# Latent attention: value products in fp32 on the two column halves of the array, in batches of four blocks, and divisors from sums made by GpSimd

## The chip, the cores and the metric

The kernel runs on one core of a Trainium2 chip. The metric is the device time of one execution in microseconds (us). Before the change it is 2091.34 us, the median of 3 runs (2090.69 to 2093.28).

TensorE (PE) does the matrix products, with its weight loads listed apart (PEld); VectorE is DVE, ScalarE is ACT, GpSimd is POOL, and SP issues most of the DMAs.

## The reference

A decoder trunk of two layers over 1024 positions, width 1024, all in fp32. Layer 0 mixes with multi-head latent attention of 12 heads, layer 1 with sliding-window attention; both have four memory cross-attention heads beside them and a dense MLP behind. The change touches the attention of layer 0 only:

```python
def causal_dense_attention(q, k, v):          # 12 heads, q and k 96 wide, v 64 wide
    ...
        sc = jnp.einsum('bqhd,bkhd->bhqk', q_blk, k,
                        preferred_element_type=jnp.float32) * scale
        mask = k_idx[None, :] <= t_idx[:, None]
        sc = jnp.where(mask[None, None], sc, NEG)
        p = jax.nn.softmax(sc, axis=-1).astype(v.dtype)
        return jnp.einsum('bhqk,bkhd->bqhd', p, v)
```

## The kernel before

**Tiling.** Scores are made transposed, keys on the partitions: a block (G, k) holds the 128 keys of tile k against up to 512 queries of half G (queries 0 to 511 for G = 0, 512 to 1023 for G = 1), less the columns that causality rules out. A head has twelve blocks: eight for G = 1 (512 columns for k = 0 to 4, then 384, 256 and 128) and four for G = 0 (512, 384, 256, 128). The list `blocks` gives their order, `seq` strings the heads together, and one loop over `n` issues for each n the scores of one block, pieces of the next heads' row maxima, and the value products of blocks that lie a few steps back (`LV` = 3 and `LB` = 5).

**Scores.** `scores` (matmuls at L1042) makes three fp32r products for each block (high by high, high by low, low by high), so that two fp32r numbers stand for one fp32. The row maximum of the head, made ahead by `row_max` (L909, one fp32r pass, reduced on DVE at L916) and turned by `max_row` (L888), rides along as a 97th row. DVE then adds the causal mask to the diagonal 128 columns of eight of the twelve blocks (L1050), and ACT takes the exponential into `p` (L1052).

**Values and divisors.** `values` (L1072) multiplies `v` by `p` and adds over k in one PSUM bank for each (head, G), `pso`. The weights are 128 wide: 64 columns of v and 64 of ones, so that row 64 of the result is the sum of the probabilities, the divisor. Blocks of G = 1 (and k = 3 of G = 0) are done "whole", in fp32, with `vf` (filled by `v_full`, a DVE copy at L1145). Blocks k = 0, 1, 2 of G = 0 are done as three fp32r products with `vh`, `vl` (made by `v_tiles`, ACT at L1014 and DVE at L1015) and with `ph`, `pl`, which ACT (L99) and DVE (L100) split from `p`. When a (head, G) is complete, ACT copies 65 rows out (L1098), and two SP DMAs send 64 of them to `qn` and the divisors to `den`.

**Division.** After heads 5, 9 and 10 `rc_split` takes reciprocals of `den` (L1131), sends them through DRAM (`rcd`, L1132) and has them broadcast to `rb` (`rc_pair`, L1124). `rc_mul` multiplies `qn` by them on DVE (L1141). For groups 0 and 1 these DMAs are issued by POOL, for group 2 by SP. The last head is divided straight from PSUM by `last_o` (L1111, L1112). Behind the loop `wo_phase` begins the output projection (`pswo`, L109 to L111), with its first four steps calling `last_o` for G = 0.

**Order.** A tile scheduler sets the order on each engine from the order of the program; on the chip each engine runs its list in order. PSUM has eight banks: six one-bank slots ("m"), for `pss`, `pso`, `psxt` and the short `psx`, and one two-bank slot ("x") for the `psx` of row tiles 4 to 7.

Of the kernel before, what the change touches and what calls it, by code (L numbers as in the profile page):

```python
# [19 lines left out]
P = 128  # L20
# [35 lines left out]
def trunk(  # L56
# [970 lines left out]
    probs, po_, masked = {}, {}, []  # L1027

    def width(G, k):
        return 512 - max(0, k - 4 * G) * P  # L1030

    def scores(h, G, k):

        qh, ql, kh, kl = bufs_[h % 3]
        c0 = 512 - width(G, k)
        ks = slice(k * P, (k + 1) * P)
        qs = slice(G * 512 + c0, G * 512 + 512)
        diag = k >= 4 * G
        ps = ps1(f"pss{h}_{G}_{k}")[:, c0:]

        def mm(o, a, b, **kw):
            return lambda: nc.tensor.matmul(o, a, b, skip_group_check=True, **kw)  # L1042

        mms = [mm(ps, kh[:, ks], qh[:, qs], start=True, stop=False)]
        mms.append(mm(ps, kh[:, ks], ql[:, qs], start=False, stop=False))
        mms.append(mm(ps, kl[:, ks], qh[:, qs], start=False, stop=True))

        def then():
            if diag:
                masked[0:1] = [nc.vector.tensor_tensor(ps[:, 0:P], ps[:, 0:P], dmaskT, ALU.add).ins]  # L1050
# [1278 lines left out]
```

## Time and profile before

| what | value |
|---|---|
| device time, median of 3 | 2091.34 us |
| profiled execution, span | 2089.8 us |
| latent attention of layer 0 in the span | about 233 to 434 us |
| one head in the middle of it | about 16.5 us |
| PE busy in that stretch of 201 us | 198.09 us |
| DVE, ACT, POOL busy in it | 156.58, 126.35, 14.00 us |

The span runs from the first to the last instruction of one profiled execution; the median is 1.5 us above it. A line of the profile names the source line, the engine, the operation, the tiles written and read and their shapes, how many instructions there were, their busy time and the mean of one, and the idle time just ahead of them with what ended it. In a timeline each row gives a start, a duration, and how many instructions of one kind in a row it groups; matmuls overlap their neighbours in such a row, so what a matmul costs is the distance between starts, not the duration printed.

### The profile page before, as it was taken

The numbers are of one execution on the slowest core, as the hardware profiler recorded it, in microseconds if no ns is written. First come the engines' busy times: TensorE is split into PE (matmuls) and PEld (weight loads), VectorE is DVE, ScalarE is ACT, GpSimd is POOL, SyncE is SP. The second block draws the span as 40 slices with busy tenths as digits, with TensorE's granted clock in tenths as the row PEclk, the third lists the DMA queues.
The fourth block names the chain that finished last, engine by engine and source line by source line (L and its number), as shares of the span: only waits on it lengthen the run. The fifth ranks groups of instructions, "written<-read, shape, count | busy, mean of one in ns | idle before, by whom it ended". The sixth has DMA issues, their size and how long they took to land.

```text
span 2089.8 us, 28906 instructions
## 1 busy us (share of the span) xinstructions
PE 2072.6 (99%) x9744; PEld 1692.2 (81%) x9744; DVE 1475.7 (71%) x2978; ACT 1109.4 (53%) x2396; POOL 148.6 (7%) x265
## 2 busy tenths in 40 slices
PE   9999999999999999999999999999999999999998
PEld 6988777778888888888888888778888888888887
DVE  8766778775977777976558534666977776976565
ACT  7554466666745544444445435766755544444453
POOL 1001001000000000000001133420000000000000
PEclk9999999999999999999999999999999999999999
DMA  6302223342444546944433534542344446944332
GB/s 225 104 1 77 63 65 93 105 149 81 142 152 150 167 152 233 332 129 152 143 118 108 146 101 124 142 130 84 128 152 164 161 144 233 324 146 156 117 121 91
DMA packets 182228, 292.86 MB, mean 140 GB/s; under 512 B 17739, under 2 KB 72128, under 8 KB 182080
## 3 DMA queue, kind: packets, MB, share of 16 engines
q1 hardware_dynamic: 175584, 272.60, 41.5%
q0 software_dynamic: 5168, 15.80, 2.1%
q10 hardware_dynamic: 1328, 2.63, 0.4%
q8 instruction: 76, 1.25, 0.2%
q14 instruction: 72, 0.59, 0.1%
HBM read 187.60 MB, written 81.44 MB: 129 GB/s over the span
## 4 chain that ended last, share of the span: by engine, by line
PE 94%; DVE 3%; ACT 1%; DMA 1%; issue 1%; SPq 0%; POOL 0%; DVEq 0%; ACTq 0%
PE psy L1903 6%; PE psy L1901 6%; PE psy L1902 6%; PE psu L1565 5%; PE psu L1564 5%; PE psu L1563 5%; PE psz L1903 4%; PE psz L1902 4%; PE psz L1901 4%; PE psv L1565 4%; PE psv L1564 4%; PE psv L1563 4%; PE pso L1072 3%; PE pss L1042 3%; PE pswo L109 3%; PE pswo L111 3%
## 5 line engine op out<-in xcount | busy, mean ns | idle before, releaser
L99 ACT ACTIVATE g<-i 128x512 fp32r<-128x512 f32 x79 | 49.9, 631 | 104.6 <-PE psy L1902 51.8
L1901 PE MATMUL psy<-g 128*128 128x512 f32 x256 | 100.1, 391 | 0.0
L1902 PE MATMUL psy<-g 128*128 128x512 f32 x256 | 99.8, 390 | 0.0
L1903 PE MATMUL psy<-g 128*128 128x512 f32 x256 | 99.8, 390 | 0.0
L1052 ACT ACTIVATE p<-pss 128x512 f32<-128x512 f32 (+2 forms) x144 | 68.7, 486 | 58.5 <-DVE pss L1050 50.0
L100 DVE TENSOR_TENSOR g<-i,g 128x512 fp32r<-128x512 f32 x79 | 55.5, 702 | 51.0 <-ACT g L99 51.0
L1072 PE MATMUL pso<-p,vf 128*128 128x512 f32 (+3 forms) x214 | 87.8, 492 | 0.0
L99 ACT ACTIVATE i<-mr 128x512 fp32r<-128x512 f32 x78 | 47.8, 629 | 73.2 <-PE psy L1902 24.5
L99 ACT ACTIVATE uh<-i 128x512 fp32r<-128x512 f32 x66 | 41.6, 630 | 82.4 <-PE psz L1902 38.4
L100 DVE TENSOR_TENSOR uh<-i,uh 128x512 fp32r<-128x512 f32 x66 | 45.6, 691 | 47.3 <-ACT uh L99 47.2
L916 DVE CUSTOM_DVE_ANT_0 psx<-psx,wide 128x1024 f32<-128x1024 f32 (+6 forms) x88 | 66.7, 760 | 14.6 <-PE psx L909 14.4
L1903 PE MATMUL psz<-g 128*128 128x512 f32 x192 | 74.8, 389 | 0.0
L1901 PE MATMUL psz<-g 128*128 128x512 f32 x192 | 74.8, 389 | 0.0
L1902 PE MATMUL psz<-g 128*128 128x512 f32 x192 | 74.8, 389 | 0.0
L1462 ACT ACTIVATE mr<-mr,gcol 128x256 f32<-128x256 f32 (+1 forms) x160 | 63.9, 477 | 13.9 <-DMA mr<-in_mlp_w_up_dram 13.9
L100 DVE TENSOR_TENSOR i<-mr,i 128x512 fp32r<-128x512 f32 x78 | 53.7, 688 | 24.7 <-ACT i L99 24.7
L1903 PEld LDWEIGHTS psy<-g 128*128 128x128 f32 x256 | 48.1, 188 | 9.9
L1902 PEld LDWEIGHTS psy<-g 128*128 128x128 f32 x256 | 48.1, 188 | 9.8
L1901 PEld LDWEIGHTS psy<-g 128*128 128x128 f32 x256 | 48.1, 188 | 9.8
L1783 DVE TENSOR_TENSOR mqq<-mqf,mqq 128x512 f32<-128x512 f32 x64 | 43.2, 687 | 18.2 <-DMA mqf<-in_mlp_w_down_dram 18.1
L1462 ACT ACTIVATE d<-d,gcol 128x256 f32<-128x256 f32 x128 | 53.6, 499 | 0.1
L2158 ACT ACTIVATE sp<-sp,sst 128x257 f32<-128x257 f32 (+1 forms) x96 | 46.5, 488 | 13.0 <-DVE sst L2156 12.7
(674 smaller groups left out, 6855.4 us busy)
## 6 DMA issues: line engine op xcount, KB each, us to landing
i<-hd SPq DMA_DIRECT2D x154, 256.0 KB
hd<-uh SPq DMA_DIRECT2D x76, 256.0 KB
hd<-ul SPq DMA_DIRECT2D x76, 256.0 KB
mr<-in_mlp_w_up_dram SPq DMA_DIRECT2D x36, 512.0 KB
hd<-x SPq DMA_DIRECT2D x72, 256.0 KB
mr<-hd SPq DMA_DIRECT2D x70, 256.0 KB
d<-in_mlp_w_up_dram SPq DMA_DIRECT2D x32, 512.0 KB
mqf<-in_mlp_w_down_dram SPq DMA_DIRECT2D x32, 512.0 KB
```

Of the source, the lines that this page charges most:

```text
L99: a = nc.scalar.activation(hi, src, AF.Copy)
L100: d = nc.vector.tensor_tensor(lo, src, f32(hi), ALU.subtract)
L916: nc.vector.tensor_tensor_reduce(o, o, k, -1.0, least, ALU.add, ALU.min, accum_out=m)
L1052: masked[1:] = [nc.scalar.activation(p[:, c0:], ps, AF.Exp, scale=SC).ins]
L1072: mms.append(lambda: nc.tensor.matmul(o, a, b, skip_group_check=True, **kw))
L1462: nc.scalar.activation(w[:, k, :], w[:, k, :], AF.Copy, scale=g_mlp[layer][:, k0 + k : k0 + k + 1])
L1563: nc.tensor.matmul(ps, wh[:, k, :], xh[:, k, :], start=p in (1, 2, 5) and k == 0, stop=False, skip_group_check=True)
L1564: nc.tensor.matmul(ps, wh[:, k, :], xl[:, k, :], start=False, stop=False, skip_group_check=True)
L1565: nc.tensor.matmul(ps, wl[:, k, :], xh[:, k, :], start=False, stop=k == 3, skip_group_check=True)
L1901: nc.tensor.matmul(ps, ah[:, j, :], bh, start=start, stop=False, skip_group_check=True)
L1902: nc.tensor.matmul(ps, ah[:, j, :], bl, start=False, stop=False, skip_group_check=True)
L1903: nc.tensor.matmul(ps, al[:, j, :], bh, start=False, stop=k == NP - 1, skip_group_check=True)
```

## The change

`p` stays in fp32 for all blocks and is kept in ten buffers. `values` takes four blocks at a time: each block's columns are cut into quarters of 256, a quarter's weights are the 64 columns of `v` alone, and the two quarters of a half go to the left and the right 64 columns of the array (`g`), taken in turns. One PSUM bank holds the head's output. The divisors come from `acc`: POOL copies and adds the blocks' probabilities (ten adds and two copies for a head), and `sums` multiplies the two halves of `acc` by 64 columns of ones. ACT copies them out and three SP DMAs send them to `den`. `evac` copies the output once for a head, 128 by 512, and issues two SP DMAs. `v_tiles`, `v_full`, the splits `ph` and `pl`, and the lags `LV` and `LB` are gone, the order in `blocks` is another, the DMAs of `rc_split` and `rc_pair` are all issued by SP, and `last_o` works on both column halves in two steps in place of four.

```diff
-    blocks = [(1, 0), (0, 0), (1, 4), (0, 1), (1, 5), (0, 2), (1, 6), (0, 3), (1, 7), (1, 1), (1, 2), (1, 3)]
+    blocks = [(1, 0), (0, 0), (1, 5), (0, 1), (1, 4), (0, 2), (1, 1), (1, 6), (1, 2), (0, 3), (1, 7), (1, 3)]
+    BATCH = 4
+    def quarters(G, c0=0):
+        return [(part ^ G, max(c0, part * 256), part * 256 + 256) for part in range(2) if c0 < part * 256 + 256]
...
-            p = at.tile([P, 512], F32, tag="p", bufs=5, name=f"p{h}_{G}_{k}")
-            if whole(h, G, k):
-                probs[(h, G, k)] = p
-                return
-            ph = at.tile([P, 512], F32R, tag="ph", bufs=3, name=f"ph{h}_{G}_{k}")
-            pl = at.tile([P, 512], F32R, tag="pl", bufs=3, name=f"pl{h}_{G}_{k}")
-            split(p[:, c0:], ph[:, c0:], pl[:, c0:])
+        p = at.tile([P, 512], F32, tag="p", bufs=10, name=f"p{h}_{G}_{k}")
...
+            if c0:
+                nc.gpsimd.tensor_copy(a[:, :c0], q[:, :c0])
+        nc.gpsimd.tensor_tensor(a[:, c0:], p[:, c0:], (a if q is None else q)[:, c0:], ALU.add)
...
-            mm(po[:, c0:], vfs[h % 2][:, k, :], probs.pop((h, G, k))[:, c0:], start=first, stop=last)
+            for g, a, b in quarters(G, col0(G, k)):
+                todo[g].append((b - a, po[g * 64 : g * 64 + 64, base + a % 256 : base + a % 256 + b - a], v[:, k, h * 64 : h * 64 + 64], p[:, a:b], g, begun))
...
+        while todo[0] or todo[1]:
+            for t in todo:
+                if t:
+                    _, o, w, r, g, begun = t.pop(0)
+                    nc.tensor.matmul(o, w, r, start=g not in begun, stop=True, skip_group_check=True)
...
-            on = at.tile([65, 512], F32, tag="on", bufs=2, name=f"on{h}_{G}")
-            nc.scalar.activation(on, po[0:65], AF.Copy)
+        on = at.tile([P, 512], F32, tag="on", bufs=2, name=f"on{h}")
+        nc.scalar.activation(on, po, AF.Copy)
...
+            nc.tensor.matmul(sp[0:64].rearrange("p (a c) -> p a c", c=256), ones, acc4[:, 0:4:3, :], start=True, stop=True, skip_group_check=True)
+            nc.tensor.matmul(sp[64:128], ones, acc[:, 256:768], start=True, stop=True, skip_group_check=True)
...
-            (nc.sync if c == 2 else nc.gpsimd).dma_start(out=rb[e * 64 : e * 64 + 64, :], in_=rc_d[c][2 * j + e, halves[i]].partition_broadcast(64))
+            nc.sync.dma_start(out=rb[e * 64 : e * 64 + 64, :], in_=rc_d[c][2 * j + e, halves[i]].partition_broadcast(64))
...
+        if n % BATCH == 1 and n > BATCH:
+            values(seq[n - 1 - BATCH : n - 1])
+            if j == 1 and h < H:
+                evac(h - 1)
+            if j == 5 and h:
+                sums(h - 1)
```

Three places show what the scheduler makes of it. Names hold the head, the half and the block (`p5_1_2` is head 5, G = 1, k = 2), and a number at the end that tells buffers apart. The first is on PE, at the end of head 5 and the start of head 6. Before:

```order
L909 MATMUL psx7_5_3582<-ckl_555,ckh_554 128x512
L909 MATMUL psx7_5_3582<-ckl_555,ckh_554 128x256
L1042 MATMUL pss6_1_0_3586<-qh0_1949,kh0_1951 128x512
L1072 MATMUL pso5_1_3465<-p5_1_1_3556,vf1_2540 128x512
L1042 MATMUL pss6_1_0_3586<-ql0_1950,kh0_1951 128x512
L1042 MATMUL pss6_1_0_3586<-qh0_1949,kl0_1952 128x512
L1042 MATMUL pss6_0_0_3603<-qh0_1949,kh0_1951 128x512
L1072 MATMUL pso5_1_3465<-p5_1_2_3569,vf1_2540 128x512
```

And after, in the same place:

```order
L1068 MATMUL pso5_1_3493<-p5_1_2_3542,v_1483 64x256
L1026 MATMUL pss6_1_0_3582<-qh0_1949,kh0_1951 128x512
L1026 MATMUL pss6_0_0_3599<-qh0_1949,kh0_1951 128x512
L1068 MATMUL pso5_1_3493<-p5_1_2_3542,v_1483 64x256
L1026 MATMUL pss6_1_5_3620<-qh0_1949,kh0_1951 128x384
L909 MATMUL psx7_3_3629<-ckl_555,ckh_554 128x512
L909 MATMUL psx7_4_3606<-ckl_555,ckh_554 128x320 x2
L1068 MATMUL pso5_1_3493<-p5_1_3_3575,v_1483 64x256
L1027 MATMUL pss6_1_0_3582<-ql0_1950,kh0_1951 128x512
L1028 MATMUL pss6_1_0_3582<-qh0_1949,kl0_1952 128x512
L1027 MATMUL pss6_0_0_3599<-ql0_1950,kh0_1951 128x512
L1028 MATMUL pss6_0_0_3599<-qh0_1949,kl0_1952 128x512
```

Whole value products of 512 columns stood between the score products; now quarters of 256 on one column half stand there one at a time, ahead of the last three quarters of the batch. The second place is on PE where the row maximum's two-bank slot changes hands in head 5. Before:

```order
L909 MATMUL psx7_7_3537<-ckl_555,ckh_554 128x512 x2
L1042 MATMUL pss5_1_7_3541<-qh2_2527,kh2_2529 128x128
L1072 MATMUL pso5_0_3481<-pl5_0_1_3473,vh1_2537 128x384
L1042 MATMUL pss5_1_7_3541<-ql2_2528,kh2_2529 128x128
L1072 MATMUL pso5_0_3481<-ph5_0_2_3500,vh1_2537 128x256
L1042 MATMUL pss5_1_7_3541<-qh2_2527,kl2_2530 128x128
L1072 MATMUL pso5_0_3481<-ph5_0_2_3500,vl1_2538 64x256
L1042 MATMUL pss5_1_1_3552<-qh2_2527,kh2_2529 128x512
L1042 MATMUL pss5_1_1_3552<-ql2_2528,kh2_2529 128x512
L1042 MATMUL pss5_1_1_3552<-qh2_2527,kl2_2530 128x512
L909 MATMUL psx7_6_3558<-ckl_555,ckh_554 128x512
```

After, from the second half of the same row tile on:

```order
L909 MATMUL psx7_7_3534<-ckl_555,ckh_554 128x512
L1068 MATMUL pso5_1_3493<-p5_1_0_3413,v_1483 64x256 x2
L1068 MATMUL pso5_1_3493<-p5_0_0_3431,v_1483 64x256 x2
L1068 MATMUL pso5_1_3493<-p5_1_5_3452,v_1483 64x256
L1068 MATMUL pso5_1_3493<-p5_0_1_3464,v_1483 64x256
L1068 MATMUL pso5_1_3493<-p5_0_1_3464,v_1483 64x128
L1068 MATMUL pso5_1_3493<-p5_1_5_3452,v_1483 64x128
L1087 MATMUL psd4_None_3502<-acc4_3242,ones_2535 64x512
L1088 MATMUL psd4_None_3502<-acc4_3242,ones_2535 64x512
```

The nine matmuls between `psx7_7` and `psx7_6` became the whole first batch with the divisors of the head before, and thirteen more matmuls (of `pss5_1_1`, `psxt7`, `pss5_1_6`, `pss5_1_2` and `pss5_0_3`) follow before `psx7_6`. The third place is on DVE at the start of head 5, behind the row maximum of tile 5. Before:

```order
L916 ISA psx6_5_3412,m8_6_3366<-psx6_5_3412,wide_2534 128x768
L916 ISA m8_6_3366 128x1
L100 TENSOR_TENSOR ckl_555<-k32_7_3424,ckl_555 96x1024
L100 TENSOR_TENSOR ckh_554<-q32_7_3423,ckh_554 96x1024
L1050 TENSOR_TENSOR pss5_0_0_3433<-pss5_0_0_3433,dmaskT_67 128x128
L916 ISA psx6_4_3445,m8_6_3366<-psx6_4_3445,wide_2534 128x640
L916 ISA m8_6_3366 128x1
L1050 TENSOR_TENSOR pss5_1_4_3449<-pss5_1_4_3449,dmaskT_67 128x128
L916 ISA psx6_3_3456,m8_6_3366<-psx6_3_3456,wide_2534 128x512
L916 ISA m8_6_3366 128x1
L100 TENSOR_TENSOR pl5_0_0_3442<-p5_0_0_3439,ph5_0_0_3441 128x512
L1050 TENSOR_TENSOR pss5_0_1_3464<-pss5_0_1_3464,dmaskT_67 128x128
```

After:

```order
L916 ISA psx6_5_3405,m8_6_3360<-psx6_5_3405,wide_2534 128x768
L916 ISA m8_6_3360 128x1
L100 TENSOR_TENSOR ckl_555<-k32_7_3417,ckl_555 96x1024
L100 TENSOR_TENSOR ckh_554<-q32_7_3416,ckh_554 96x1024
L1030 TENSOR_TENSOR pss5_0_0_3426<-pss5_0_0_3426,dmaskT_67 128x128
L916 ISA psx6_4_3433,m8_6_3360<-psx6_4_3433,wide_2534 128x640
L916 ISA m8_6_3360 128x1
L1030 TENSOR_TENSOR pss5_1_5_3447<-pss5_1_5_3447,dmaskT_67 128x128
L916 ISA psx6_3_3456,m8_6_3360<-psx6_3_3456,wide_2534 128x512
L916 ISA m8_6_3360 128x1
L1030 TENSOR_TENSOR pss5_0_1_3459<-pss5_0_1_3459,dmaskT_67 128x128
```

The splits of head 7's queries and keys (`ckl`, `ckh`) stand ahead of the same mask as before; the subtraction for `pl` is gone.

## Rows read from the trace of the kernel before

**Rows 1.** The page's first part: engine, busy us, share of span, instructions.

```profile
PE 2072.6 (99%) x9744; PEld 1692.2 (81%) x9744; DVE 1475.7 (71%) x2978; ACT 1109.4 (53%) x2396; POOL 148.6 (7%) x265
```

**Rows 2.** Two stretches: length, PE, PEld, DVE, ACT, POOL busy (x), PEclk, DMA, GB/s.

```profile
233.00:434.00 201.00, 198.09 (x904) 145.00 (x903) 156.58 (x386) 126.35 (x257) 14.00 (x28) 1.00 0.35 91
434.00:452.00 18.00, 17.83 (x71) 13.97 (x71) 17.34 (x33) 10.82 (x21) 1.12 (x2) 0.91 0.38 135
```

**Rows 3.** What PE waited for, 233 to 434 us: total, times, longest.

```profile
PE psx L909 <- DVE m L916: 1.2, 2, 0.7
PE psx L909 <- ACT p L1052: 0.6, 1, 0.6
PE pso L1072 <- ACT ph L99: 0.4, 1, 0.4
PE pswo L109 <- ACT x L99: 0.3, 1, 0.3
PE pss L1042 <- ACT p L1052: 0.2, 1, 0.2
```

**Rows 4.** PE timeline in two places, start, duration, line, tiles, count.

```profile
299.44 1.02 PE L1072 MATMUL pso<-p,vf 128*128 128x512 f32 x2
299.90 1.25 PE L1042 MATMUL pss<-ckh,ckl 97*128 97x512 f32 x3
300.98 1.02 PE L1072 MATMUL pso<-p,vf 128*128 128x512 f32 x2
...
425.54 0.39 PE L1042 MATMUL pss<-qh,kl 97*128 97x512 f32 x1
425.77 0.40 PE L1042 MATMUL pss<-qh,kh 97*128 97x512 f32 x1
426.00 0.39 PE L1042 MATMUL pss<-ql,kh 97*128 97x512 f32 x1
```

**Rows 5.** PE timeline of a cross-attention value product, 64 columns of the array.

```profile
151.67 0.28 PE L448 MATMUL pscx<-kml,qc 128*128 128x256 f32 x1
151.88 1.95 PE L474 MATMUL psco<-cpT,vm0b 128*64 128x256 f32 x16
153.75 1.09 PE L459 MATMUL pscT<-ident,cps 128*128 128x128 f32 x8
```

**Rows 6.** PE timeline of sliding-window value products on 64 columns, in two places.

```profile
1329.21 0.28 PE L2152 MATMUL psw<-kl,q 128*128 128x256 f32 x1
1329.41 1.51 PE L2204 MATMUL pswo<-spT,v 128*64 128x384 f32 x8
1330.86 0.88 PE L2186 MATMUL pswt<-ident,sp 128*128 128x128 f32 x6
...
1352.78 0.86 PE L2204 MATMUL pswo<-spT,v 128*64 128x384 f32 x2
1353.57 0.55 PE L2186 MATMUL pswt<-ident,sp 128*128 128x128 f32 x3
```

**Rows 7.** PE timeline between two row-maximum tiles in the middle of a head.

```profile
311.59 0.86 PE L1042 MATMUL pss<-ckh,ckl 97*128 97x512 f32 x3
312.42 0.67 PE L909 MATMUL psx<-kh,qh 96*128 96x512 f32 x2
312.93 0.59 PE L1072 MATMUL pso<-p,vf 128*128 128x256 f32 x2
```

**Rows 8.** DVE groups by shape, 233 to 434 us: busy, mean ns, idle before.

```profile
L1050 DVE TENSOR_TENSOR pss<-pss,dmaskT 128x128 f32<-128x128 f32 x96 | 29.0, 303 | 6.9 <-PE pss L1042 6.7
L916 DVE CUSTOM_DVE_ANT_0 psx<-psx,wide 128x1024 f32<-128x1024 f32 x11 | 13.5, 1228 | 1.9 <-PE psx L909 1.8
L100 DVE TENSOR_TENSOR ql<-q,qh 96x1024 fp32r<-96x1024 f32 x7 | 8.5, 1214 | 0.0
L100 DVE TENSOR_TENSOR pl<-p,ph 128x512 fp32r<-128x512 f32 x12 | 8.2, 688 | 1.5 <-ACT ph L99 1.5
L100 DVE TENSOR_TENSOR pl<-p,ph 128x384 fp32r<-128x384 f32 x12 | 6.7, 555 | 4.2 <-ACT ph L99 4.1
L1145 DVE COPY vf<-v 128x512 f32<-128x512 f32 x12 | 5.4, 448 | 0.0
L1015 DVE TENSOR_TENSOR vl<-v,vh 128x256 fp32r<-128x256 f32 x12 | 5.0, 420 | 4.0 <-ACT vh L1014 4.0
L100 DVE TENSOR_TENSOR pl<-p,ph 128x256 fp32r<-128x256 f32 x12 | 5.0, 416 | 3.9 <-ACT ph L99 3.9
```

**Rows 9.** POOL groups by shape, whole span.

```profile
L2176 POOL TENSOR_TENSOR sp<-sp,sst 128x768 f32<-128x768 f32 x28 | 42.0, 1499 | 29.4 <-DVE sst L2175 29.3
...
L1124 POOL DMA_DIRECT2D rb<-rcd x20 | 10.5, 535 | 16.3 <-DVE qn L1141 10.9 <-DMA rcd<-rc 2.9 <-DVE pss L1050 2.5
...
L2176 POOL TENSOR_TENSOR sp<-sp,sst 128x384 f32<-128x384 f32 x4 | 3.3, 829 | 23.3 <-DVE sst L2175 22.3 <-PE psw L2152 1.0
...
L1132 POOL DMA_DIRECT2D rcd<-rc x2 | 1.1, 551 | 156.0 <-DVE ml L100 108.2 <-DVE pl L100 47.8
```

**Rows 10.** Timeline of DVE, in two places.

```profile
1327.19 1.22 DVE L100 TENSOR_TENSOR woq<-wor,woq 128x1024 fp32r<-128x1024 f32 x1
...
1328.40 1.20 DVE L100 TENSOR_TENSOR woq<-wor,woq 128x1024 fp32r<-128x1024 f32 x1
...
1330.11 0.49 DVE L2156 CUSTOM_DVE_ANT_0 sp<-psw,df,sinks_b 128x256 f32<-128x256 f32 x1
...
1350.14 2.27 DVE L100 TENSOR_TENSOR woq<-wor,woq 128x1024 fp32r<-128x1024 f32 x1
```

**Rows 11.** Timeline of POOL, in the same two places.

```profile
1328.57 2.36 POOL L2176 TENSOR_TENSOR sp<-sp,sst 128x768 f32<-128x768 f32 x1 [2.24 <-DVE sst L2175]
...
1349.86 1.47 POOL L2176 TENSOR_TENSOR sp<-sp,sst 128x768 f32<-128x768 f32 x1
```

**Rows 12.** PE timeline where the output projection begins.

```profile
435.55 0.61 PE L109 MATMUL pswo<-woq,x 128*128 128x512 f32 x1
435.96 0.63 PE L110 MATMUL pswo<-woq,x 128*128 128x512 f32 x1
436.39 0.63 PE L111 MATMUL pswo<-woq,x 128*128 128x512 f32 x1
...
439.31 0.40 PE L109 MATMUL pswo<-woq,x 128*128 128x512 f32 x1
439.54 0.40 PE L110 MATMUL pswo<-woq,x 128*128 128x512 f32 x1
```

More of the change, by code (lines that the diff above doesn't have):

```diff
@@ L1109, in last_o @@
+    def last_o(G, tmp, js=range(2)):
+        po, sp = po_[(H - 1, G)][0], sp_[G]
         for j in js:
             c = slice(j * P, (j + 1) * P)
-            nc.vector.reciprocal(tmp[:, c], po[64:128, c])
-            nc.vector.tensor_tensor(qn[5][64:128, G * 512 + j * P : G * 512 + (j + 1) * P], po[0:64, c], tmp[:, c], ALU.mult)
+            nc.vector.reciprocal(tmp[:, c], sp[:, c])
+            for g, a, _ in quarters(G):
+                r = slice(g * 64, g * 64 + 64)
+                t0 = G * 512 + a + j * P
+                nc.vector.tensor_tensor(qn[5][64:128, t0 : t0 + P], po[r, c], tmp[r, c], ALU.mult)
@@ L1165, in trunk @@
     muls = iter(())
-    for n in range(len(seq) + LB):
-        ms, mv, then = [], [], []
+    for n in range(len(seq) + 2):
         if n < len(seq):
-            ms, then_s = scores(*seq[n])
-        for lag, late in ((LB, True), (LV, False)):
-            if 0 <= n - lag < len(seq):
-                a, b = values(*seq[n - lag], late)
-                mv += a
-                then.append(b)
-        mix = []
-        if ms and mv and P in [width(*seq[n - lag][1:]) for lag in (0, LV, LB)]:
-            while ms and mv:
-                mix += [ms.pop(0), mv.pop(0)]
-        for f in mix + ms:
-            f()
-        if n < len(seq):
-            then_s()
+            scores(*seq[n])
         for g, i in ahead.get(n, ()):
@@ L1201, in trunk @@
                     head_tiles(2)
-        for f in mv:
-            f()
-        for f in then:
-            f()
+        if n % BATCH == 1 and n > BATCH:
[4 more added lines that the diff above has]
+                sums(h - 1)
+            if n == len(seq) - 3:
+                sums(H - 1, 1)
+                last_o(1, at.tile([P, 256], F32, tag="on", bufs=2, name="rq1"))
         if n % 2 or n > 11 * NB:
@@ L1424, in wo_phase @@
                     oo[p + 1] += osp(p + 1, (1,))
[L1425 removed]
+                if layer == 0 and half == 0 and p < 2:
                     if p == 0:
[L1427 removed]
+                        od = m.t("i39")[:, 0, :]
                     last_o(0, od, [p])
```

143 lines of the change are left out of this document (60 added, 83 removed).

## The prediction

> **What bounds the kernel now.** Read the page's first part [rows 1]: PE is busy for 2072.6 of 2089.8 us, every other engine for 71% or less. Then the stage: in the 201 us of the latent attention PE is busy for 198.1 at full clock, DVE for 156.6, ACT for 126.4, POOL for 14 [rows 2]. So time there follows PE's list of matmuls, and what other engines save counts only where PE waits. Named waits are few: 1.2 us on row-maximum slots that DVE gives back late, 0.8 on the exponential, and 0.7 at the stage's end [rows 3]. "Busy" hides shorter stalls, because a matmul's printed duration overlaps its neighbours'; these are read from distances between starts. The last thing to see is that POOL is idle, and that the change gives it work that reads what DVE and ACT use. The end is the span's: behind the stage comes a long chain of PE work, so a microsecond saved on PE here is one saved in all.
>
> **Value products, PE.** Prices before [rows 4]: from one fp32 block of 512 columns to the next, with three fp32r score passes between, 300.98 - 299.44 = 1.54 us; a pass is 425.77 - 425.54 = 0.23; the block is 1.54 - 0.69 = 0.85. A head has 3456 fp32 columns (6.75 blocks, 5.74 us) and 3 x 1152 = 3456 fp32r columns (6.75 passes, 1.55 us): 7.29. Eleven such heads and a last one (6.5 blocks, 7.5 passes, 7.25) make 87.4 us.
>
> Prices after: the cross attention has such products already, eight of 256 columns, four on each half. They take 153.75 - 151.88 = 1.87 us [rows 5]; at the full array's price eight would take 8 x 0.425 = 3.4, so the halves do run side by side. The sliding window's four of 384 columns take 1.45 [rows 6]. Pairs of 1024 and 768 columns in all, so a column of a pair costs (1.87 - 1.45)/256 = 1.64 ns, and 1.87 - 1.68 = 0.19 is left as the price of leaving the half mode. Entering costs 0.21 where a 256-column pass takes 0.12, so 0.09 more: 0.28 for a visit. A matmul behind a stall is also slow itself (896 columns in 0.51 instead of 0.40) [rows 7]; if that holds behind a visit it is 0.38. I take 0.33. A product alone on its half gains nothing: 0.79 for 384 columns [rows 6].
>
> The order shows what the scheduler does with the batches. The first stands unbroken with the divisors (896 + 512 paired columns), the second too (768), but the third is cut in six of the heads: three lone quarters of 256 between score products, then 256 + 128. That head has 3328 columns in six visits: 5.46 + 1.98 = 7.44 us, against 7.29 before. Unbroken it would have 2816 in three visits, 5.61. Over all heads I count 65 visits and 40,576 columns, a lone one counted whole: 66.5 + 21.5 = 88.0 us. **The term is 88.0 - 87.4 = +0.6**, and -2.7 or +3.8 with the visit at 0.28 or 0.38. The halved arrays give away to visits, lone quarters and the new divisor products what they win.
>
> The Trainium skill ("TensorEngine Tiling (Array Packing)", Theoretical Speedup and Key Properties) promises up to 2x where one side is 64 or less, and says that a change of tiling mode drains the engine. Rows 5 agree with the first for a pair and rows 6 with the second; by the 2x alone the products would take 5632 / 2 columns x 12 x 1.64 ns = 55.4 us, 32 less than before.
>
> **Row maxima.** The two-bank slot goes from `psx_7` to `psx_6` while DVE needs 1.23 us for the first [rows 8]. PE gets there too early in each head: three score passes take 0.83 instead of 0.69, and the 896 columns 0.51 instead of 0.40 [rows 7]: 0.25 a head, in the nine heads that the named waits don't count already, 2.2 us. After, a visit of 1408 columns (2.6 us) and thirteen matmuls (2.0) stand between the two, so the slot is free in time: **-2.2**. The two named waits of 1.2 on the same slot go the same way; the 0.8 on the exponential may stay in part, since the last block of a batch is used two blocks after its scores, where the kernel before has three. I take **-1.6** for both, between 0 and -2.0.
>
> **DVE and ACT.** DVE loses `pl` (8.2 + 6.7 + 5.0), `vf` (5.4) and `vl` (5.0), 30 us or 2.5 a head [rows 8]; ACT loses `ph` and `vh` and has as many copies out of PSUM as before. Neither was the bound, so this counts nothing beyond the waits above. The narrow score products now stand three in a row where a value product stood between two; I put nothing down for that, within 1.5 us either way.
>
> **POOL.** Adds of 768 columns take 1.50 us and of 384 take 0.83 [rows 9], so 1.75 ns a column and 0.16: about 1.05 for 512. Ten adds of 3584 columns are 7.9 us and two copies about 0.6, 8.5 us of a head of 16.5: half busy. The sums are used five blocks into the next head, some 7 us after the last add can begin, so they are no wait by themselves.
>
> But POOL and DVE hold each other up. A DVE subtraction of 128 x 1024 took 2.27 us beside a POOL add that began 0.28 us earlier, and 1.22 alone; a POOL add took 2.36 instead of 1.50, while DVE's work on PSUM, 0.49 us at 1330.11, went on beside it [rows 9 to 11]. So masks and reductions (PSUM inputs) should be safe, and the two splits of 96 x 1024 in each head (1.21 us each) [rows 8] can each be late by up to one add, 1.05. Behind them on DVE wait the first mask of the head and the row-maximum reductions, and behind the mask the exponential and the first batch. From `psx_5` to the point where that mask has its scores PE has about 4.3 us of work; DVE needs for the reduction and two splits 0.97 + 0.14 + 2 x 1.21 = 3.5. The slack of 0.8 covers most of one collision, and the blocks behind the mask have another 1 to 2 us before their batch. I take **0** with +9 as the other end. The Trainium skill ("GPSIMD Engine Reference", Specifications and Performance versus the Vector engine) speaks against this part: POOL shares its SBUF interfaces with VectorE and is slower at elementwise work. The collisions in rows 10 and 11 agree; its verdict would be the slower rival below.
>
> **DMAs.** POOL issued 22 small DMAs for the division [rows 9]; now SP does, ahead of the row maximum's own row for a later head, and behind them on SP wait the loads of the head tiles. A head has five SP DMAs for output and divisors where it had four. A wait for a reciprocal that holds SP up would delay one head's start: 0 to +1.5, I take **+0.3**.
>
> **The end.** The last value products and the three last visits lie among `pswo`. The waits of 0.7 there [rows 3] may be filled by longer work, and PE's clock, which there was the lower of its levels for eight passes (0.43 apart from 435.96 to 436.39, 0.23 at 439.31) [rows 12], may fall again: **0**, within 2 either way.
>
> **Sum.** +0.6 - 2.2 - 1.6 + 0.3 = -2.9: a span of 2086.9 us. The median stands 1.5 above the profiled span, so I forecast 2088.4, 0.14% below before. About 0.2% (4.2 us) is what a measurement of this kernel can tell from no change, so the likeliest is no change that shows, and it is near the edge.
>
> **Rivals.** (a) Faster by about 12: PE's list, at the prices of rows 4, comes to some 190 us of the 203 up to the first third product of `pswo` (436.39) [rows 12]. If relief of DVE and ACT and a freed bank of PSUM remove most of that rest, not only the named waits, the time is 2079. For it: 30 us less on DVE. Against: few waits have DVE's name. (b) Faster by about 35: every quarter runs beside another and entering and leaving are hidden, so the term is 55.4 - 87.4 = -32 and the sum 2056; the order speaks against it, as the lone quarters and 65 visits are in it. It is the ceiling that the Trainium skill ("TensorEngine Tiling (Array Packing)", Theoretical Speedup) names. (c) Slower: POOL and DVE collide on both splits of each head, the mask comes up to 1.3 us late, and PE waits about 0.8 of that in eleven heads: +9 with the gain of 2.9 lost in part, 2099. It decides from a delay above the slack of 0.8 us. For it: POOL is half busy, so two collisions of two are likely in some heads. Against: the first batch comes late enough. (d) Slower by the end: one more fall of the clock, eight passes x 0.19 = 1.5, and lone visits there, +5 in all, 2096. (e) The halves don't run side by side for this form: 5632 columns a head x 12 x 1.64 ns = 111 us and visits, +45; rows 5 are against it.
>
> **How the numbers follow.** The sum 0.57 (0.21 of it faster by over 0.2%, 0.33 within, 0.03 slower), (a) 0.16, (b) 0.02, (c) 0.17, (d) 0.06 (half within), (e) 0.02. Faster 0.39, same 0.36, slower 0.25. The range from 2078 to 2100 leaves out (b), (e) and the far ends of (a) and (c).
>
> **What would show it.** In the profile after: visits of 64 columns with 0.28 to 0.38 us beyond their columns and about 7.4 us a head in a cut head; no 0.14 ahead of `psx_6`; DVE below 130 us in the stage; POOL adds at about 1.05 us for 512 columns; splits at 1.2 (right) or above 2 (rival c), with PE's waits on `p` or `psx` behind them. I am wrong if a cut head takes clearly less than 16 us or more than 17.

## The result and the profile after

The changed kernel takes 2097.23 us (median of 6 runs, 2096.0 to 2104.38) against 2091.18 before: a ratio of 1.0035, interval 1.0024 to 1.0046. I had forecast 2088.4, a little faster; it is slower by 6 us. The profiled execution has a span of 2094.9 us, 5.1 above the 2089.8 of before.

The window of the stage (columns as in [rows 2]):

```profile
233.00:434.00 201.00, 194.35 (x1090) 127.36 (x1088) 142.38 (x317) 101.89 (x199) 134.13 (x142) 0.98 0.33 83
```

PE is idle for 6.7 us of the 201, where before it was idle for 2.9, and its clock is 0.98 in the mean. DVE lost 14 us, not the 30 that were taken off it. POOL went from 14 to 134. What PE waited for, 233 to 441 us:

```profile
PE pso L1068 <- ACT p L1032: 3.1, 3, 1.9
PE pswo L109 <- ACT x L99: 2.1, 1, 2.1
PE psx L909 <- DVE m L916: 1.4, 3, 0.6
PE pss L1026 <- DVE m L916: 1.2, 2, 0.6
PE psd L1092 <- POOL acc L1045: 1.0, 1, 1.0
```

That is 8.8 us of named waits; the kernel before has 2.9 in the same 208 us, the 2.7 of [rows 3] and 0.2 behind them. The groups of DVE and POOL in the same stretch show where most of DVE's 16 us came back from (columns as in [rows 8]):

```profile
L100 DVE TENSOR_TENSOR ql<-q,qh 96x1024 fp32r<-96x1024 f32 x7 | 11.8, 1679 | 0.0
L100 DVE TENSOR_TENSOR kl<-k,kh 96x1024 fp32r<-96x1024 f32 x7 | 10.6, 1511 | 0.1
L100 DVE TENSOR_TENSOR woq<-wor,woq 128x1024 fp32r<-128x1024 f32 x4 | 8.4, 2111 | 0.0
L1139 DVE TENSOR_TENSOR qn<-rb,qn 128x512 f32<-128x512 f32 x8 | 7.7, 978 | 3.4 <-DMA rb<-rcd 3.4
L1045 POOL TENSOR_TENSOR acc<-p,acc 128x512 f32<-128x512 f32 x47 | 69.2, 1473 | 18.7 <-ACT mh L99 10.7 <-ACT p L1032 6.6
```

The multiplications by `rb` before, 233 to 434 us:

```profile
L1141 DVE TENSOR_TENSOR qn<-rb,qn 128x512 f32<-128x512 f32 x8 | 5.5, 689 | 6.1 <-DMA rb<-rcd 5.9 <-issue 0.2
```

The splits of 96 x 1024 were 1.21 us each [rows 8] and are 1.68 and 1.51 in the mean in these two rows; those of `woq` were 1.22 and are 2.11; the multiplications by `rb` were 0.69 and are 0.98. The masks and the reductions, which read PSUM, kept their durations (303 and 1244 ns against 303 and 1228). An add of 512 columns takes 1.47 us in the mean, and 1.27 or 1.28 with no two-input instruction of DVE beside it (at 250.25 and 388.58), where I had estimated 1.05.

**Where the time went.** The transposes of the row maxima (L888) mark the heads. In the middle:

```profile
310.77 0.27 PE L888 MATMUL psxt<-ident,m 128*8 128x128 f32 x1
327.30 0.27 PE L888 MATMUL psxt<-ident,m 128*8 128x128 f32 x1
...
360.30 0.28 PE L888 MATMUL psxt<-ident,m 128*8 128x128 f32 x1
381.82 0.27 PE L888 MATMUL psxt<-ident,m 128*8 128x128 f32 x1
398.10 0.27 PE L888 MATMUL psxt<-ident,m 128*8 128x128 f32 x1
```

A head in the middle takes 327.30 - 310.77 = 16.53 us; before it takes 16.48 (308.73 to 325.21 there). So the middle is level. The loss lies in single places. One is 1.3 us up to the third head: the first interval is level (20.67 against 20.72), the next two are 13.79 and 15.71 against 12.83 and 15.28. The other is the interval that ends in head 8, which is 21.52 where before it was 17.04:

```profile
358.57 0.27 PE L888 MATMUL psxt<-ident,m 128*8 128x128 f32 x1
375.61 0.28 PE L888 MATMUL psxt<-ident,m 128*8 128x128 f32 x1
```

The interval ahead of it gives 0.4 of that back and the one behind it 1.4; the last one adds 0.8, and from there to the end of the span it is 0.5 less than before. Ahead of the first transpose it is 0.6 more.

The start, PE, DVE and POOL in this order:

```profile
243.93 1.08 PE L1068 MATMUL pso<-p,v 128*64 128x256 f32 x8
246.96 0.65 PE L1068 MATMUL pso<-p,v 128*64 128x256 f32 x4 [1.94 <-ACT p L1032]
```

```profile
242.85 1.22 DVE L100 TENSOR_TENSOR ql<-q,qh 96x1024 fp32r<-96x1024 f32 x1
243.99 2.29 DVE L100 TENSOR_TENSOR kl<-k,kh 96x1024 fp32r<-96x1024 f32 x1
246.20 0.28 DVE L1030 TENSOR_TENSOR pss<-pss,dmaskT 128x128 f32<-128x128 f32 x1
```

```profile
242.99 2.21 POOL L1045 TENSOR_TENSOR acc<-p,acc 128x512 f32<-128x512 f32 x1 [1.42 <-ACT p L1032]
```

The add begins 0.14 us behind the first split and ends only at 245.20; the second split ends at 246.28, a good 1.0 late; the mask waits behind it, the exponential behind the mask, and PE stands in the middle of a batch for 1.94 us. Without adds (e4, below) this wait is 0.9, so about 1.0 of it is the adds'. It lies in the first interval, which is level with before all the same. The loss in the next two stays in e4 (13.80 and 15.56), so it isn't this collision that makes them longer. Head 8, PE:

```profile
370.68 0.51 PE L1026 MATMUL pss<-qh,kh 97*128 97x512 f32 x1 [0.60 <-DVE m L916]
371.75 0.38 PE L909 MATMUL psx<-kh,qh 96*128 96x256 f32 x1 [0.57 <-DVE m L916]
372.72 0.58 PE L1026 MATMUL pss<-qh,kh 97*128 97x256 f32 x1 [0.58 <-DVE m L916]
373.10 0.63 PE L1027 MATMUL pss<-ql,kh 97*128 97x512 f32 x1
373.53 0.63 PE L1028 MATMUL pss<-qh,kl 97*128 97x512 f32 x1
```

and SP:

```profile
364.14 2.78 SPq L1122 DMA_DIRECT2D rb<-rcd  x4
366.97 0.70 SPq L896 DMA_DIRECT2D ql<-ml  x1
```

PE does first passes and row maxima of head 8 ahead of its second passes, runs out of PSUM slots, and waits three times for DVE, whose list holds multiplications among the reductions. Behind these stops the passes are 0.43 us apart where they are 0.23 at full clock: the granted clock is 0.50 from 373.1 to 377.4, the lower of its two levels. The row that the second passes need stands on SP behind four DMAs of `rb`; that PE waits for that row itself is not shown, as its stops name DVE.

These stops are not collisions. POOL does nothing from 370 to 373.1 us, the two multiplications there take 0.69 each, and e4, without adds, has the same three stops (0.61, 0.58 and 0.58). Its third one, and a window behind it:

```profile
370.40 0.39 PE L1026 MATMUL pss<-qh,kh 97*128 97x256 f32 x1 [0.58 <-DVE m L916]
```

```profile
372.00:376.00 4.00, 4.00 (x20) 2.81 (x20) 1.88 (x8) 3.58 (x7) 0.00 (x0) 0.57 0.00 0
```

There the clock falls some 1.8 us later, and the rest of the interval is 1.5 us shorter. What the adds themselves cost in head 8 stands ahead of the stops, on ACT and PE of the changed kernel:

```profile
366.11 0.77 ACT L1032 ACTIVATE p<-pss 128x128 f32<-128x128 f32 x2 [3.56 <-POOL acc L1045]
366.93 0.86 PE L1068 MATMUL pso<-p,v 128*64 128x256 f32 x6 [0.96 <-ACT p L1032]
```

An exponential waits 3.56 us for an add. The only thing of an add that it can need is a buffer of `p` that the add still reads, so this is a second way for POOL to cost time, beside the longer instructions of DVE.

### The profile page after: what moved, and what is told of

It reads as the page before. It is cut to its first block, busy times and chain, and to the rows that moved or that the text cites. A ratio compares the mean times of both kernels' runs of the same rounds, so it can differ in the third digit from the quotient of the medians.

```text
span 2094.9 us, 29501 instructions
## 1 busy us (share of the span) xinstructions
PE 2070.5 (99%) x9951; PEld 1674.6 (80%) x9951; DVE 1461.6 (70%) x2913; ACT 1087.8 (52%) x2347; POOL 271.1 (13%) x383
## 3 DMA queue, kind: packets, MB, share of 16 engines
q8 instruction: 78, 1.28, 0.3%
## 4 chain that ended last, share of the span: by engine, by line
PE 94%; ACT 2%; DVE 2%; issue 1%; DMA 1%; POOL 1%; ACTq 0%; SPq 0%; DVEq 0%; POOLq 0%
PE psy L1879 6%; PE psy L1878 6%; PE psy L1880 6%; PE psu L1542 5%; PE psu L1541 5%; PE psu L1540 5%; PE psz L1879 4%; PE psz L1878 4%; PE psz L1880 4%; PE psv L1542 4%; PE psv L1541 4%; PE psv L1540 4%; PE pswo L109 3%; PE pswo L111 3%; PE pswo L110 3%; PE pso L1068 3%
## 5 line engine op out<-in xcount | busy, mean ns | idle before, releaser
L1045 POOL TENSOR_TENSOR acc<-p,acc 128x512 f32<-128x512 f32 (+3 forms) x96 | 102.9, 1085 | 28.5 <-ACT p L1032 15.3
L1032 ACT ACTIVATE p<-pss 128x512 f32<-128x512 f32 (+3 forms) x144 | 66.8, 490 | 67.9 <-DVE pss L1030 33.6
L916 DVE CUSTOM_DVE_ANT_0 psx<-psx,wide 128x1024 f32<-128x1024 f32 (+5 forms) x88 | 66.3, 762 | 15.4 <-PE psx L909 14.8
L1068 PE MATMUL pso<-p,v 128*64 128x256 f32 (+1 forms) x480 | 70.8, 374 | 3.1 <-ACT p L1032 3.1
L1998 POOL TENSOR_TENSOR wsr<-wsr,gcol 128x1024 f32<-128x1024 f32 x12 | 23.1, 1927 | 344.7 <-ACT i L99 274.9
L1068 PEld LDWEIGHTS pso<-p,v 128*64 128x64 f32 x480 | 34.4, 138 | 32.5 <-issue 13.5
L1880 PEld LDWEIGHTS psy<-g 128*128 128x128 f32 x256 | 48.1, 188 | 10.0
L1878 PEld LDWEIGHTS psy<-g 128*128 128x128 f32 x256 | 48.1, 188 | 9.9
```

What stands on the lines that cost most here:

```text
L916: nc.vector.tensor_tensor_reduce(o, o, k, -1.0, least, ALU.add, ALU.min, accum_out=m)
L1045: nc.gpsimd.tensor_tensor(a[:, c0:], p[:, c0:], (a if q is None else q)[:, c0:], ALU.add)
L1068: nc.tensor.matmul(o, w, r, start=g not in begun, stop=True, skip_group_check=True)
L1878: nc.tensor.matmul(ps, ah[:, j, :], bh, start=start, stop=False, skip_group_check=True)
L1880: nc.tensor.matmul(ps, al[:, j, :], bh, start=False, stop=k == NP - 1, skip_group_check=True)
```

## The experiments

In each pair of numbers the first is the kernel's median, the second that of the kernel before on the same chip. Edits are to the changed kernel unless the text says otherwise.

**The DMAs back on POOL (e1), on SP in the kernel before (e2).**

```diff
-            nc.sync.dma_start(out=rb[...], ...)
+            (nc.sync if c == 2 else nc.gpsimd).dma_start(out=rb[...], ...)     # e1; rcd alike; e2 the reverse
```

> The changed kernel with one part undone: the DMAs of rcd and rb for groups 0 and 1 are issued by POOL again, as in the kernel before. In the changed kernel head 8 takes 21.5 us from one transpose of row maxima to the next where its neighbours take 16.5. Theory 1 (SP): eight small rb DMAs stand on SP ahead of the row that the score products of head 8 need, so head 8's second and third passes start late and the clock falls; then head 8 takes 16.5 to 17.5 us here and the time is about 4 us less, near 2093. Theory 2 (DVE and POOL): the multiplications by rb on DVE collide with POOL's adds and give PSUM back late; then head 8 stays above 20 us and the time stays within 1 us of 2097.

> The kernel before with that one part alone: rcd and rb of all groups issued by SP. Theory 1 (SP): a head around the multiplications gets longer by 2 to 5 us, the time is 2093 to 2096. Theory 2 (DVE and POOL): POOL has no adds here, so the time stays within 1 us of 2091.2.

Measured: e1 2097.76 against 2090.83 (ratio 1.0034, 1.0021 to 1.0046), the interval at head 8 24.4 us; e2 2093.68 against 2090.83 (1.0011, 1.0003 to 1.0020), which is inside theory 1's 2093 to 2096. The 24.4 is read from a profiled execution of 2102.35 us, 4.6 above the median, with a granted clock of 0.50 from 370 to 380 us; e6 below, with its DMAs on POOL too, has 18.3 there. So the time decides: e1 is level with the changed kernel. The first theory, that SP's queue alone is the cause, falls: with the DMAs on POOL they stand behind adds, and now DVE waits for them:

```profile
366.02 1.19 DVE L1139 TENSOR_TENSOR qn<-rb,qn 128x512 f32<-128x512 f32 x1 [2.02 <-DMA rb<-rcd]
```

**Whole batches (e3), and both edits (e6).**

```diff
+        lastmm[0:] = [nc.tensor.matmul(ps, kl[:, ks], qh[:, qs], ...).ins]
...
-            values(seq[n - 1 - BATCH : n - 1])
+            with tc.issue_after(lastmm[0]):
+                values(seq[n - 1 - BATCH : n - 1])
```

> The changed kernel with the value products of a batch traced behind the last score product, so that the scheduler leaves most batches whole: 48 visits to the column halves in place of 65, and 37,250 paired columns in place of 39,550 (a lone one counted whole). Theory A (a visit costs 0.33 us beyond its columns, and PE is the bound): 17 visits x 0.33 + 2300 columns x 1.64 ns = 9.4 us less, near 2088, and a head in the middle takes about 15.7 us in place of 16.53. Theory B (the scheduler cut batches because their inputs come late; PE then waits instead): the head stays at 16.4 to 16.6 with waits on p or on the row of maxima, and the time stays within 2 us of 2097.

> Both edits together: rcd and rb by POOL, and whole batches (46 visits). Theories 1 and A: the gains add up, 4 + 10 us less than the changed kernel, near 2083, which is below the kernel before. Theories 2 and B: no gain from either, 2096 to 2098.

Measured: e3 2097.33 against 2090.83 (1.0036, 1.0022 to 1.0050), e6 2096.93 (1.0026, 1.0016 to 1.0037). In the traces e3 has 48 visits where the changed kernel has 65, and its head in the middle is 16.46: theory B. Its first three intervals are 4.3 us longer than the changed kernel's, and what is behind the middle gives that back. e6 has no gain from either edit. The chain of waits of e3 from 304 to 311 us (start, length, what) shows what took the gain:

```profile
305.83 1.08 DVE kl L100
306.91 2.23 DVE ql L100
309.14 0.22 DVE pss L1030
309.36 0.02 issue
309.38 0.61 ACT p L1032
309.98 0.04 issue
310.03 0.50 PE pss L1026
```

Two splits, the second beside an add, then mask, exponential, and the PSUM slot that PE needs. This is the chain of my rival (c), and it binds as soon as PE has less to do.

**Adds left out (e4), and with whole batches (e5); adds put into the kernel before (e7).**

```diff
-        nc.gpsimd.tensor_tensor(a[:, c0:], p[:, c0:], (a if q is None else q)[:, c0:], ALU.add)     # and the copies
+            nc.gpsimd.memset(acc_["acc"], 1.0)      # once; e4, e5
...
+            nc.gpsimd.tensor_tensor(acc_[h][:, c0:], p[:, c0:], wide[0][:, c0:512], ALU.add)     # e7, kernel before
```

> The changed kernel without POOL's copies and adds: acc is a constant, so the sums of probabilities, and with them the divisors, are left out; the products with ones, the copies and the DMAs of the divisors stay. Theory C (collision): in the changed kernel DVE's splits of 96 x 1024 took 1.39 to 2.03 us in the mean; here 1.22, and what was lost at the start of the stage (1.3 us by head 3), at head 8 and at the end comes back in good part: 2091 to 2094. A head in the middle stays at 16.4 to 16.5, since it is bound by PE's visits. Rival (PE alone is the bound and POOL costs nothing): within 1.5 us of 2097.

> Whole batches, as in the run before of that name, and POOL's copies and adds left out (the divisors are wrong constants). In the run with whole batches a head in the middle stayed at 16.46 us, with PE waiting 0.5 us behind a chain of two splits on DVE (1.08 and 2.23 us), a mask and an exponential. Theory C (that chain is long because the second split stands beside an add): the split takes 1.22, the wait goes, the head falls to 15.4 to 15.9 us, and the time to about 2085 to 2089. Rival (the chain, or the row of maxima by DMA, is as long without POOL): the head stays within 0.2 us of 16.46.

> The kernel before with POOL's work alone added: for each block one POOL add of p and a constant into a scratch tile that nothing reads (12 adds and 4608 columns a head against 10 adds, two copies and 3584 columns; one rb buffer instead of two makes the room). Theory C: DVE's splits and subtractions with two inputs in SBUF get longer by 0.5 to 1 us each, DVE was busier here than in the changed kernel, so PE waits: a head in the middle goes from 16.48 to 17 or more, and the time to 2097 to 2110. Rival (POOL's adds are hidden): heads stay at 16.48 and the time within 2 us of 2091.

Measured: e4 2091.04 against 2090.72 (1.0000, 0.9991 to 1.0010), 6.2 less than the changed kernel. Its splits are at 1.21 to 1.22 us again; the middle head stays at 16.53; what came back is at the start (1.2 us), at head 8 (2.6, the interval is 18.91: 1.1 ahead of the three stops and 1.5 behind them at the lower clock) and behind the last transpose (1.8, with the wait of 1.0 for `acc` gone). e5: 2089.32 (0.9994, 0.9985 to 1.0003), the middle head 15.87, at or just above the upper end of what was expected: whole batches do gain 0.66 us a head in the middle, once no add stands beside the splits. e7: 2128.54 (1.0181, 1.0165 to 1.0196), far above the 2097 to 2110 expected, with heads of 18.92 in place of 16.48. From its lines, 265 to 350 us:

```profile
L100 DVE TENSOR_TENSOR ql<-q,qh 96x1024 fp32r<-96x1024 f32 x3 | 6.9, 2296 | 0.0
L100 DVE TENSOR_TENSOR pl<-p,ph 128x512 fp32r<-128x512 f32 x4 | 5.3, 1331 | 0.0
L100 DVE TENSOR_TENSOR pl<-p,ph 128x384 fp32r<-128x384 f32 x4 | 5.0, 1244 | 2.6 <-ACT ph L99 2.6
...
L100 DVE TENSOR_TENSOR kl<-k,kh 96x1024 fp32r<-96x1024 f32 x3 | 3.7, 1217 | 0.0
```

The same work of DVE, 0.69 to 1.33 and 1.21 to 2.30 us, with nothing but POOL's adds beside it (the `rb` buffer that the edit takes away is not in use in this window). Here the adds hold nobody up by being late themselves: POOL is busy for 64.29 of the 85 us, waits 18.4 us for exponentials, and no wait that is listed names it. The first split of a pair keeps 1.22 and the second takes 2.30, as in the changed kernel: the add slips in between two.

**The division (e8, e9, e10).** e8 and e9 leave out the division of heads 0 to 9 in the changed kernel and in the kernel before; e10 spreads it.

```diff
-        for c in range(3):
+        for c in range(2, 3):      # e8, e9
...
-        if n % 2 or n > 11 * NB:
+        if j in (6, 11) or n > 11 * NB:      # e10; rc_pair issued two ahead of its use
```

> The changed kernel without the division of heads 0 to 9: the reciprocals, their DMAs and the multiplications of groups 0 and 1 are left out. Theory D (head 8 is long, 21.5 us against 16.5, because the multiplications and their DMAs stand in the queues of DVE and SP): head 8 takes 16.5 us, and the time falls by 4 to 6 us to 2091 to 2093. Rival (head 8 is long for a reason in the score chain itself, as at heads 1 and 2): head 8 stays above 19 us.

> The kernel before without the division of heads 0 to 9 (reciprocals, their DMAs and multiplications of groups 0 and 1 left out), for comparison with the changed kernel without it, 2089.2. Theory D (the division costs the changed kernel more than the kernel before, since there the multiplications collide with POOL and the DMAs stand on SP): here only the 2.2 us by which heads 7 to 10 exceed 16.48 go, 2088 to 2089, so that the two kernels without division are within 1.5 us. Rival (the division costs both the same 8 us): 2083.

> The changed kernel with the multiplications spread out: two for a head (blocks 6 and 11) in place of one for every second block, and the DMAs of rb issued two ahead of their use in place of all at once. Theory D: head 8 falls from 21.5 us to 16.5 to 18 and the time by 3 to 5 us, to 2092 to 2094. Rival (any multiplication there costs what it costs): 2096 to 2098.

Measured: e8 2089.15 against 2090.72 (0.9993, 0.9983 to 1.0003), 8.1 less than the changed kernel; e9 2090.47 against 2090.77 (0.9998, 0.9989 to 1.0008). The same ten multiplications and 22 DMAs that cost the kernel before 0.3 us cost the changed one 8.1; the profile of e8 has head 8 at 16.52, 5.0 less, and most of the rest in the last interval (14.93 against 17.50) and behind it. For e9 a fall by 2.2 us, to 2088 to 2089, was expected; 0.3 came, inside its interval. e10: 2093.22 (1.0013, 1.0003 to 1.0022), so half of the 8.1 is their place. The interval at head 8 there is 14.94:

```profile
362.45 0.28 PE L888 MATMUL psxt<-ident,m 128*8 128x128 f32 x1
377.39 0.27 PE L888 MATMUL psxt<-ident,m 128*8 128x128 f32 x1
```

Two profiles differ where the edit doesn't reach, too. The first two intervals of e10 are 2.4 us longer than the changed kernel's, with the same matmuls and the same stop of 1.9 us at the start. The stretch behind that stop, in the changed kernel and in e10:

```profile
245.00:250.00 5.00, 3.06 (x19) 1.65 (x17) 4.65 (x13) 2.06 (x6) 3.04 (x5) 1.00 0.61 131
```

```profile
245.00:250.00 5.00, 3.34 (x11) 2.13 (x12) 3.28 (x11) 1.57 (x5) 2.44 (x4) 0.61 0.59 126
```

The granted clock is 1.00 in one and 0.61 in the other. So a single interval of one profile can be 2 us off for this alone; the medians are what the theories are judged by.

**Do the two add up (e15, e16)?** e15 is e4 and e8 together, e16 e4 and e10.

> The changed kernel with POOL's adds left out (constant divisors) and the division of heads 0 to 9 left out too. Alone the first gave 2091.0 (6.2 less than the changed kernel), the second 2089.2 (8.1 less). If the two costs are one (the multiplications are dear because they stand beside adds), 2087 to 2089. If they are separate, they add up: 2083. The kernel before without division, 2090.5, is what to compare it with: what is left between the two is what the value products on halves give by themselves.

> The changed kernel with POOL's adds left out (constant divisors) and the multiplications spread as in the run of that name, which with adds gave 2093.2. If the remaining cost of the spread version is POOL's, this falls by 4 to 6 us to 2087 to 2089; if spreading had already taken what the adds cost, 2091 to 2093.

Measured: e15 2084.69 against 2091.20 (0.9968, 0.9955 to 0.9980), e16 2088.44 (0.9986, 0.9976 to 0.9995). The two alone are 6.2 and 8.1, together 12.5: for the most part two costs. The 1.8 us that would be one are less than these runs can tell apart (the interval of the changed kernel's ratio alone is 4.6 us wide). e16 is 4.8 below e10, so spreading had not taken what the adds cost. Without either the changed kernel is 5.8 below the kernel before without division (e9).

**Splits elsewhere (e11 to e14).** e11 has whole batches, and each later head's two subtractions stand behind the reductions of row tiles 7 and 6; e12 has the spread division besides; e13 and e14 hold batches whole only from head 2 on, with the multiplications at blocks 2 and 4, or 0 and 3.

```diff
-                head_tiles(h + 2)
+                low = head_tiles(h + 2, True)      # ACT's part now
+            if h and j in (7, 9) and h + 2 < H:
+                with tc.issue_after(reduced[0]):
+                    nc.vector.tensor_tensor(*low.pop(0), ALU.subtract)
...
+            with tc.issue_after(lastmm[0] if n > 2 * NB else masked[1]):      # e13, e14
-        if n % 2 or n > 11 * NB:
+        if j in (2, 4) or n > 11 * NB:      # e13; e14 (0, 3); e12 (6, 11)
```

> Whole batches, and the two subtractions of the split of each later head's queries and keys moved on DVE from the head's start to a place behind the reductions of row tiles 7 and 6, where the next mask is not urgent. POOL's adds are as in the changed kernel. Theory C (with whole batches the head is bound by a chain in which one split stands beside an add just ahead of a mask): the chain is cut without taking POOL's work away, a head in the middle falls from 16.46 to 15.7 to 16.0, and the time from 2097.3 to 2091 to 2094. Rival (POOL's work costs wherever the splits stand): heads stay above 16.3.

> Both: whole batches with the splits moved, and the multiplications spread. Theories C and D together: heads in the middle at 15.7 to 16.0 and head 8 below 18, the time 2086 to 2090, below the kernel before. Rivals: 2094 to 2098.

> As the run with splits moved and multiplications spread, but batches are held whole only from head 2 on, so that the first two heads keep value products as work to put between the row maxima, and the multiplications stand at blocks 2 and 4 of a head, away from the moved splits. Theory E (all that is left of the loss lies at three places, the first two heads, the heads with multiplications and the end, and each is a wait on DVE's or POOL's order, not the price of the value products): the first two heads come back to within 2 us of the kernel before, heads 7 to 10 to 16.5 or less, the middle stays at 15.6, and the time is 2085 to 2091. Rival F (POOL's adds cost wherever room is made, as more work of DVE collides): 2094 to 2100.

> The same with the multiplications at blocks 0 and 3. Theory E: within 2 us of the run before it, both below the kernel before or level with it. Rival F: 2094 to 2100; a difference of more than 3 us between the two would say that the place of the multiplications is what decides.

Measured: e11 2098.49 against 2090.77 (1.0034, 1.0023 to 1.0045), e12 2099.97 (1.0037, 1.0023 to 1.0050), e13 2098.37 against 2090.83 (1.0030, 1.0019 to 1.0041), e14 2094.38 (1.0018, 1.0009 to 1.0027). In the middle e11 is what was expected, two rows of L892 there and its window, to be read beside that of e3:

```profile
296.28 0.27 PE L892 MATMUL psxt<-ident,m 128*8 128x128 f32 x1
311.86 0.27 PE L892 MATMUL psxt<-ident,m 128*8 128x128 f32 x1
```

```profile
265.00:350.00 85.00, 85.00 (x505) 58.89 (x503) 61.20 (x147) 44.89 (x91) 65.56 (x64) 1.00 0.30 66
```

```profile
265.00:350.00 85.00, 82.89 (x481) 55.12 (x481) 57.41 (x137) 45.79 (x90) 60.43 (x63) 1.00 0.29 65
```

A head of 15.58 us, 0.9 below the kernel before, with all of POOL's adds and PE (the first busy column) never idle, where in e3 it was idle for 2.1 us. So in the middle the place of two instructions on DVE decides, not POOL's work as such. But the time did not follow: the first two heads of e11 lost 4.9 us against the kernel before (PE waited 3.0 us for DVE's row maxima, with no value products free to do meanwhile, and the granted clock was 0.76 in the mean from 248 to 262), and its head 8 was 21.6 again. e12 had head 8 at 17.5, as expected, in a profile 4.8 below its median, and missed the 2086 to 2090 by 10 us. e13 and e14 differ only in where the multiplications stand: by 4 us in the medians, though their intervals overlap, and in head 8 by 20.9 against 17.3. Up to the last transpose e14 is 2.0 us ahead of the kernel before and e13 0.8 behind it; from there to the end of the span they take 4.3 and 5.6 more. Theory E held for the middle; its first two heads, 2.1 and 2.5 us above the kernel before, came close to the 2 it named; head 8 and the time it missed. No version that computes everything beat the kernel before.

## Why the prediction was wrong, step by step

**Value products (+0.6): right in kind, too small.** The lone quarters stand where the order said. Two rows of after:

```profile
299.26 0.65 PE L1068 MATMUL pso<-p,v 128*64 128x256 f32 x2
299.84 0.73 PE L1026 MATMUL pss<-ckh,ckl 97*128 97x512 f32 x2
300.50 0.65 PE L1068 MATMUL pso<-p,v 128*64 128x256 f32 x2
```

A quarter of 0.42 us takes 0.58 to the next matmul, and the two passes behind it 0.66 in place of 0.46 with the next entrance: 0.36 for a visit, near my upper end of 0.38. With 65 visits that makes the term +2.5 in place of +0.6, an estimate from these rows. The cut head came out at 16.53, inside the 16 to 17 that I had named. The gain of whole batches bears on the price from the other side, without settling it: in e11 a middle head has four visits for six and 256 paired columns fewer (0.42 us), which at 0.36 a visit would save 1.14, and it saves 0.95 (0.27 a visit).

**Row maxima (-2.2 and -1.6).** No wait of PE on the slot is listed from 300 to 340 us; the 0.3 a head that the products cost more by the price above would have taken the place of the 0.25 that I had put on it, hence 16.53 beside 16.48. The named waits did not go: 8.8 us for 2.9, for the reasons of the next two steps.

**POOL (0): the step that failed.** I had the mechanism (rival c), its rows [rows 10, 11] and its price for one collision (1.05; the second split took 1.08 more), but I weighed it in the middle heads only, where the slack of 0.8 us and the batch behind it cover one collision. That part held: the head there is 16.53 with and without adds. What I left out is that the cover isn't there at the start of the stage, beside the multiplications by `rb` (two inputs in SBUF as well, 0.69 to 0.98) and at the end, and that adds which are late hold up others: an exponential for 3.56 us in head 8, PE for 1.0 at the end. Taken out alone, the adds give 6.2 us back. The time lies near rival (c)'s 2099, but not in its way: that rival had PE wait 0.8 us in eleven heads, and the middle heads are level. DVE's 142 us in the stage, where I had named below 130, shows the same miss. The Trainium skill ("GPSIMD Engine Reference", Specifications) names this contention, and e7 shows what 12 adds a head cost the kernel before: 37.8 us.

**DMAs (+0.3): the second step that failed.** I priced the move to SP as a delay of one head's start. It is part of a knot, and my sum had no term for the division itself: it is worth 8.1 us (e8) with adds, with late DMAs, and with PE at its lower clock for 4.3 us behind three stops for DVE. Either queue is bad (e1), spreading saves 4.0 (e10), and e2 shows that the move to SP by itself costs the kernel before some 2.9.

**DVE and ACT (nothing beyond the waits) and the end (0): open.** With adds and division out of the way the change gains 5.8 us (e15 against e9), where my sum without those steps said 3.2. It gains in the last two intervals and behind them, and not in the middle (16.53 against 16.48); I had put the end at 0. That it is the relief of DVE and ACT that gives this is not shown.

So the sum reads: -5.8, +4.5 for the adds (e8 less e15), +7.8 for the division with adds (8.1 less the 0.3 that it costs before): +6.5 against a measured +6.1. It closes because its terms are differences of the same runs, so it gives sizes and proves no cause. What stays open is the end of the stage: in e13 and e14 it takes 5.6 and 4.3 us more than before from the last transpose on, with PE's largest waits on an exponential (2.4 and 1.6) and on the last head's reciprocals (2.2 each) and a granted clock of 0.89 and 0.92 from 400 to 445 us (0.96 before), and I have no run that separates these. Open, too, is what makes the clock fall: the lower level stands behind the stops in order of time, but behind the same three stops it began at once in the changed kernel and 1.8 us later in e4, and behind the same stop at the start it came in e10's profile and not in the changed kernel's.

## What to carry to other kernels

Price work that is moved to GpSimd by what it does to VectorE's instructions with two inputs in SBUF, and look for these where there is no slack (start, end, one-off work), not only in the steady loop. When the bound engine is relieved, the next chain is often one instruction away: here moving two subtractions behind work that wasn't urgent was worth 0.9 us for a head in the middle (16.46 to 15.58), which whole batches alone had not gained. It did not make the kernel faster, since the first heads and head 8 lost that again. Work of a few microseconds that every variant carries along (here the division) can cost 0.3 or 8 us by what stands beside it.

## What the runs showed of the hardware that I had not expected

A VectorE subtraction and a GpSimd add that meet wait for each other as whole instructions, in turns: of two splits in a row the first kept 1.22 us and the second took 2.29 or 2.30, in all six pairs of the changed kernel up to 336 us that follow each other directly, and the add took 2.21 at the start where one without such an instruction beside it took 1.27. There it ended 1.13 us behind the first split, and the second split ended 1.08 behind it. And three stops of 0.57 to 0.60 us on PE, 1.75 in all, were followed by 4.3 us at a granted clock of 0.50; work of that length takes some 2.3 us at full clock (0.23 in place of 0.43 a pass), so the lower clock about doubled the loss.
